# Which gate is worked out by seven products: one second gate goes back to the ordinary product, and the sums it needed are formed beside it

## The chip, the core and the metric

The kernel runs on one core of one Trainium2 chip. The metric is the time of one execution in microseconds (us) on the device. The core has a matrix engine, TensorE (PE in the profile, its weight loads PEld), a vector engine (DVE), a scalar engine (ACT), GpSimd (POOL) and SyncE (SP). Each works through its own instructions in a fixed order and waits for the others through semaphores. SP issues nearly all loads from memory here, in the order of its queue; POOL issues a few more.

## The reference, cut to what matters

One decoder layer on 512 tokens of width 1024. The normalised input `h` is projected to everything that three mixers need, and to three gates:

```
z, xbc, dt_raw, q, k, v, u, gates = split(h @ w_in)
y_ssd  = state_space_branch(z, xbc, dt_raw) @ w_ssd_out
y_attn = attention_branch(q, k, v) @ w_attn_out
y_pool = (multi_scale_pool(u, w_pool_mix) * pool_scale) @ w_pool_out
g_ssd, g_attn, g_pool = split(sigmoid(gates))
x = x + g1 * ((g_ssd * y_ssd + g_attn * y_attn + g_pool * y_pool) @ w_out)
x = x + g2 * (square(relu(norm(x) @ w_ff1)) @ w_ff2)
```

`multi_scale_pool` subtracts each value from its mean over the last 2, 4, 8 or 16 tokens (four groups of 256 channels) and multiplies each group by its own 256x256 matrix of `w_pool_mix`.

## The kernel before, in words

**Layout.** Activations lie with channels on the 128 partitions and the 512 tokens along the free axis; 1024 channels are eight such blocks. A product of 1024x512 weights with them is a chunk; each gate has two chunks, so GS, GA and GP (state-space, attention, pooled) have a first and a second gate each.

**Precision.** Every operand is a sum of a high part and a low part. ACT casts a weight tile to get the high part `wh` (L279 or L786), DVE subtracts to get the low part `wl` (L279 or L787), and PE forms three products: low by high, high by high, high by low (lines L293 to L295, or L811).

**An ordinary chunk** (`gemm_feat`) streams four weight tiles of 128x1024 through `wstream`; each serves two of the eight blocks. The loads go to a ring of four buffers (`raws`), the two parts to a ring of three pairs (`wsp`). A chunk is 8 blocks x 4 output blocks x 3 = 96 matmuls with 512 columns.

**A chunk by seven products** (`seven_products`) treats inputs, weights and tokens as 2x2 blocks and needs seven half-size products instead of eight: 7 x 4 x 2 x 3 = 168 matmuls with 256 columns. For it DVE also builds sums of weights (L793 to L796, into the buffers tagged L0, L1, N0, N1 of the pool `exp`, each of which exists once) and sums of the input (`input_sums`). The latter come in four pieces of work, each of two additions of whole blocks (L753, L754), four of half blocks (L755 to L758) and the split of the two results into high and low parts (L320 on ACT, L321 on DVE). The input sums are kept and serve every seven-product gate that follows.

**Side work.** What is not a chunk's own work waits in a list, `side`. After each weight tile of an ordinary chunk, and twice in a seven-product one, `tick` takes one entry from that list and emits it after that tile's two split instructions. `rest(n)` puts n empty entries in it, `call` one function, and `flush` empties it.

**The stretch in question.** After the attention branch the program forms the two chunks of `u` (`pool(0)`, `pool(1)`: the chunk, then the running means on DVE), then the state-space branch's first gate GS 0, its projection `project` with `w_ssd_out` chunk 0, its second gate GS 1, the second projection, and then both pooled gates GP 0 and GP 1 with theirs. `mix_weights(n)` loads two of the four 256x256 matrices into one `raws` buffer and splits them into the `exp` buffers L0, N0 (n = 0) or L1, N1 (n = 1). `pool_mix(gi)` multiplies group gi on PE (12 matmuls), scales it on ACT (L1141) and DVE (L1142), and POOL stores it in memory (L1146); `again` loads all of it back (L1263) once the blocks of the state-space branch have become free.

**What sets the order.** A scheduler orders each engine's instructions at build time, from the order in which the code emits them. Weight loads and splits are moved ahead by `high_priority(offset=AHEAD)`, evacuations by a smaller amount; nothing is reordered on the chip.

## Time and profile before

| what | us |
|---|---|
| median of 3 runs | 1106.65 (1105.22 to 1106.88) |
| the profiled execution | 1104.65 |
| span of its trace | 1102.9 |
| PE busy | 1087.0 (99%) |
| DVE busy | 761.6 (69%) |
| ACT busy | 536.9 (49%) |

The span runs from the first to the last recorded instruction of the profiled execution; the 1.75 us between 1102.9 and 1104.65 lie around it. Times inside the trace count from the start of the span. Matmuls are pipelined: a row's duration is its latency, and neighbours start closer together than that, so the pace is read from starts or from a stretch with its count. "Idle before" names what ended the wait ahead of an instruction.

### The profile page before, as it was taken

The page shows a single profiled execution, that of the slowest core. Times are in us where ns is not written, and L with a number is a line of the kernel's source. Part 1 is how long each engine was busy: PE and PEld are TensorE (multiplying, and loading weights), DVE is VectorE, ACT ScalarE, POOL GpSimd, SP SyncE. Part 2 cuts the span into 40 slices and gives each one's busy share as a digit, 9 for nine tenths or more (in the row PEclk, how much of TensorE's full clock was granted, in tenths as well). Part 3 has the DMA queues.
Part 4 walks back from the last instruction along what each step waited for, and adds up shares of the span by engine and source line. Part 5 has one row for each costly group of instructions (what it writes and reads, how often), then busy time and mean ns, then how long its engine had stood idle before and what let it go on. Part 6 is the DMA issues. An engine that isn't in the chain of part 4 may idle for free.

```text
span 1102.9 us, 15616 instructions
## 1 busy us (share of the span) xinstructions
PE 1087.0 (99%) x6022; PEld 937.8 (85%) x6022; DVE 761.6 (69%) x1441; ACT 536.9 (49%) x877; POOL 29.2 (3%) x58
## 2 busy tenths in 40 slices
PE   8999999999999999999988999999999999999998
PEld 7878888888887888888877899899889989989987
DVE  8955746683777956678777557476797587687664
ACT  8965864643545942835425245363344334335330
POOL 0000000000000000000110200000000000000000
PEclk9999999999999999999998999999999999999999
DMA  9723143555644342223534542560224134133032
GB/s 346 296 96 100 65 162 123 176 169 182 203 151 156 102 134 99 93 77 96 191 114 132 172 155 71 178 229 1 77 58 136 64 108 134 56 116 135 20 115 77
DMA packets 49230, 142.42 MB, mean 129 GB/s; under 512 B 5874, under 2 KB 6642, under 8 KB 49156
## 3 DMA queue, kind: packets, MB, share of 16 engines
q1 hardware_dynamic: 43088, 126.08, 34.5%
q0 software_dynamic: 5344, 14.16, 4.2%
q10 hardware_dynamic: 724, 1.18, 0.3%
q8 instruction: 47, 0.77, 0.3%
q14 instruction: 27, 0.22, 0.1%
HBM read 135.08 MB, written 6.32 MB: 128 GB/s over the span
## 4 chain that ended last, share of the span: by engine, by line
PE 79%; issue 16%; DVE 2%; DMA 1%; POOL 1%; ACT 0%; SPq 0%; POOLq 0%; DVEq 0%; ACTq 0%
PE psacc L293 18%; PE psacc L295 18%; PE psacc L294 18%; PE psacc L811 16%; PE psacc L533 4%; PE psS L612 1%; PE pso L728 1%; PE pso L726 1%; POOL pool L1146 1%; PE psqT L591 0%; PE pskT L596 0%; PE pspT L709 0%; DMA xT<-in_x_dram 0%; DMA pool<-pooll 0%; POOL M L1044 0%
## 5 line engine op out<-in xcount | busy, mean ns | idle before, releaser
L279 DVE TENSOR_TENSOR wl<-raw,wh 128x1024 fp32r<-128x1024 f32 x128 | 156.2, 1221 | 138.3 <-ACT wh L279 132.8
L279 ACT CAST wh<-raw 128x1024 fp32r<-128x1024 f32 x128 | 134.2, 1049 | 208.8 <-PE psacc L294 118.6
L293 PE MATMUL psacc<-hl,wh 128*128 128x512 f32 x320 | 128.8, 403 | 0.2 <-ACT pT L710 0.2
L294 PE MATMUL psacc<-hh,wh 128*128 128x512 f32 x320 | 124.6, 390 | 0.0
L295 PE MATMUL psacc<-hh,wl 128*128 128x512 f32 x320 | 124.5, 390 | 0.0
L293 PE MATMUL psacc<-al,wh 128*128 128x512 f32 (+1 forms) x260 | 100.4, 386 | 0.0
L294 PE MATMUL psacc<-ah,wh 128*128 128x512 f32 (+1 forms) x260 | 100.4, 386 | 0.0
L295 PE MATMUL psacc<-ah,wl 128*128 128x512 f32 (+1 forms) x260 | 100.3, 386 | 0.0
L293 PE MATMUL psacc<-wl,rh 128*128 128x512 f32 x192 | 77.4, 403 | 0.0
L295 PE MATMUL psacc<-wh,rl 128*128 128x512 f32 x192 | 75.2, 392 | 0.0
L294 PE MATMUL psacc<-wh,rh 128*128 128x512 f32 x192 | 75.2, 392 | 0.0
L293 PEld LDWEIGHTS psacc<-hl,wh 128*128 128x128 f32 x320 | 60.1, 188 | 13.4 <-issue 1.2
L294 PEld LDWEIGHTS psacc<-hh,wh 128*128 128x128 f32 x320 | 60.2, 188 | 13.3 <-issue 1.4
L295 PEld LDWEIGHTS psacc<-hh,wl 128*128 128x128 f32 x320 | 60.1, 188 | 12.9
L787 DVE TENSOR_TENSOR wl<-rawl,wh 128x512 fp32r<-128x512 f32 (+1 forms) x36 | 33.7, 954 | 35.6 <-ACT wh L786 35.6
L1441 DVE SCALAR_TENSOR_TENSOR xr<-psacc,modv,xr 128x512 f32<-128x512 f32 (+1 forms) x65 | 44.7, 738 | 18.7 <-PE psacc L295 18.7
L295 PEld LDWEIGHTS psacc<-ah,wl 128*128 128x128 f32 x260 | 48.8, 188 | 9.9
L293 PEld LDWEIGHTS psacc<-al,wh 128*128 128x128 f32 x260 | 48.9, 188 | 9.7
L294 PEld LDWEIGHTS psacc<-ah,wh 128*128 128x128 f32 x260 | 48.9, 188 | 9.6
L786 ACT CAST wh<-rawl 128x512 fp32r<-128x512 f32 (+1 forms) x36 | 29.2, 833 | 51.3 <-PE psacc L294 28.7
L786 ACT CAST wh<-wsum 128x1024 fp32r<-128x1024 f32 x18 | 19.0, 1053 | 72.0 <-PE psacc L294 69.5
L811 PE MATMUL psacc<-txl,wh 128*128 128x256 f32 x144 | 42.0, 292 | 4.4 <-DVE txl L321 4.4
(423 smaller groups left out, 2746.5 us busy)
## 6 DMA issues: line engine op xcount, KB each, us to landing
raw<-in_w_in_dram SPq DMA_DIRECT2D x74, 512.0 KB, 3.6
raw<-in_w_ff_dram SPq DMA_DIRECT2D x52, 512.0 KB, 3.8
wa<-in_w_ada_dram SPq DMA_DIRECT2D x64, 256.0 KB, 3.5
wada<-in_w_ada_dram SPq DMA_DIRECT2D x14, 512.0 KB, 7.8
rawl<-in_w_ff_dram SPq DMA_DIRECT2D x12, 512.0 KB, 3.5
wst<-in_w_in_dram SPq DMA_DIRECT2D x16, 256.0 KB, 7.8
M<-prow POOLq DMA_DIRECT2D x16, 256.0 KB, 3.7
raw<-in_w_ssd_out_dram SPq DMA_DIRECT2D x8, 512.0 KB, 3.6
```

The lines of the kernel that those rows point to most:

```text
L279: edges[:] = S.copy(wh, raw), V.tensor_tensor(wl, raw, wh.bitcast(F32), ALU.subtract)
L293: mm(ps, lhsT=wh, rhs=xl, start=first, stop=False)
L294: mm(ps, lhsT=wh, rhs=xh, start=False, stop=False)
L295: mm(ps, lhsT=wl, rhs=xh, start=False, stop=last)
L533: mm(ps[j], lhsT=t[:, j, :], rhs=w, start=first, stop=last)
L612: mm(so[b], lhsT=qT[:, b * P : (b + 1) * P], rhs=kT[:, (b + 1) * P - n : (b + 1) * P], start=True, stop=True)
L726: mm(od, lhsT=vs[kb][:, hs], rhs=pT[b // 2][:, cs : cs + P], start=(b == 0), stop=False, skip_group_check=True)
L728: mm(ov[:, b, :], lhsT=vs[b][:, hs], rhs=pT[0][:, b * P : (b + 1) * P], start=False, stop=(gi == 2 and b == 3), skip_group_check=True)
L786: S.copy(h, x)
L787: V.tensor_tensor(l, x, h.bitcast(F32), ALU.subtract)
L811: mm(o, lhsT=x[:, cs], rhs=y, start=first and k == 0 and j == 0 and n == 0, stop=k == 3 and n == 2, skip_group_check=True)
L1441: V.scalar_tensor_tensor(xT[d][:, ts], p[:, : ts.stop - ts.start], modv[:, 3, d : d + 1], xT[d][:, ts], ALU.mult, ALU.add)
```

## The change

The state-space branch's second gate becomes an ordinary chunk; the two pooled gates stay the only gates by seven products. The four pieces of input sums move from "between GS 0 and GS 1" to the four ticks of that ordinary chunk. Around it, the empty entries go, one of them stays, and the pooled branch's matrices and mixing are queued in another order.

```
-    for half in range(2):
-        call(mix_weights, half)
-        pool(half)
-        rest(2)
-        call(pool_mix, 2 * half)
-        if half == 0:
-            call(pool_mix, 1)
-    side.append(lambda: (pool_mix(3), sums[0]()))
-    side.extend(sums[1:])
+
+    pool(0)
+    call(mix_weights, 0)
+    pool(1)
+    call(pool_mix, 0)
+    side.append(lambda: (mix_weights(1), pool_mix(1)))
+    rest(1)
+    call(pool_mix, 2)
+    call(pool_mix, 3)
     sg = gate(GS, 0)
     project(a["w_ssd_out"], 8, 0, yh, yl, sg)
     flush()
-    sg = gate(GS, 1, tq)
+    side.extend(sums)
+    sg = gate(GS, 1)
     project(a["w_ssd_out"], 8, 1, yh, yl, sg)
+    flush()
```

What the scheduler makes of it is seen at three places. On PE, at the point where GS 1 begins (`psmix` and `psacc` are accumulators; `pdh`, `pdl` a group's means; `wmL`, `wmN` the parts of a mixing matrix; `ynh`, `ynl` the state-space result), before:

```order
L295 MATMUL psmix_5234<-pdh_4836,wmN_5088 128x512
L293 MATMUL psmix_5234<-pdl_4855,wmL_5087 128x512
L294 MATMUL psmix_5234<-pdh_4854,wmL_5087 128x512
L295 MATMUL psmix_5234<-pdh_4854,wmN_5088 128x512
L811 MATMUL psacc_5345<-hl_254,wh_5329 128x256
L811 MATMUL psacc_5345<-hh_246,wh_5329 128x256
```

The same six places now:

```order
L293 MATMUL psacc_5090<-ynl_4744,wh_5213 128x512
L294 MATMUL psacc_5090<-ynh_4743,wh_5213 128x512
L295 MATMUL psacc_5090<-ynh_4743,wl_5214 128x512
L293 MATMUL psacc_5249<-hl_254,wh_5255 128x512
L294 MATMUL psacc_5249<-hh_246,wh_5255 128x512
L295 MATMUL psacc_5249<-hh_246,wl_5256 128x512
```

The mixing of groups 2 and 3 stood right ahead of GS 1 and is gone from there: group 0 is now mixed after the first weight tile of GS 0, group 1 after its second, group 2 at its end, and group 3 after the first tile of the projection. The number of matmuls between the starts of GS 0 and GS 1 is the same, 240.

On SP, the loads from the third tile of the first projection on (`raw` and `rawl` with `in_w_in` behind GS 0 are gate weights; L777 loads the left half of a seven-product gate's weights into tags L0 and L1, L778 the right half), before:

```order
L286 DMA raw_5121<-in_w_ssd_out_dram 128x1024
L286 DMA raw_5151<-in_w_ssd_out_dram 128x1024
L778 DMA raw_5322<-in_w_in_dram 128x1024
L778 DMA raw_5326<-in_w_in_dram 128x1024
L777 DMA rawl_5321<-in_w_in_dram 128x1024
L286 DMA raw_5572<-in_w_ssd_out_dram 128x1024
L286 DMA raw_5602<-in_w_ssd_out_dram 128x1024
L777 DMA rawl_5325<-in_w_in_dram 128x1024
L777 DMA rawl_5732<-in_w_in_dram 128x1024
```

And now:

```order
L777 DMA rawl_5617<-in_w_in_dram 128x1024
L286 DMA raw_5211<-in_w_ssd_out_dram 128x1024
L286 DMA raw_5253<-in_w_in_dram 128x1024
L286 DMA raw_5301<-in_w_in_dram 128x1024
L286 DMA raw_5349<-in_w_in_dram 128x1024
L286 DMA raw_5397<-in_w_in_dram 128x1024
L777 DMA rawl_5621<-in_w_in_dram 128x1024
L286 DMA raw_5457<-in_w_ssd_out_dram 128x1024
L286 DMA raw_5487<-in_w_ssd_out_dram 128x1024
L286 DMA raw_5517<-in_w_ssd_out_dram 128x1024
L286 DMA raw_5547<-in_w_ssd_out_dram 128x1024
L778 DMA raw_5618<-in_w_in_dram 128x1024
```

The left half of GP 0's weights (5617, 5621) is now asked for a whole gate and projection ahead of its use; four ordinary tiles of GS 1 (5253 to 5397) stand where GS 1's halves stood.

On DVE, in the middle of the second gate's stretch, before:

```order
L787 TENSOR_TENSOR wl_5330<-rawl_5325,wh_5329 128x512
L794 TENSOR_TENSOR rawl_5325<-rawl_5325 128x2x256
L795 TENSOR_TENSOR wsum_5340<-wsum_5340,rawl_5325 128x2x256
L755 TENSOR_TENSOR tq_5269<-tq_5267 128x256
L796 TENSOR_TENSOR rawl_5325<-raw_5326,wsum_5340 128x2x256
L756 TENSOR_TENSOR tq_5269<-tq_5268,tq_5269 128x256
L787 TENSOR_TENSOR wl_5402<-wsum_5340,wh_5401 128x1024
```

And now, from the second tile of GS 1 on (`sg` is a gate; L884 multiplies it with the projection, L891 adds it to the sum of branches):

```order
L279 TENSOR_TENSOR wl_5304<-raw_5301,wh_5303 128x1024
L753 TENSOR_TENSOR tq_5331<-hh_247,hl_255 128x512
L754 TENSOR_TENSOR tq_5332<-hh_251,hl_259 128x512
L755 TENSOR_TENSOR tq_5333<-tq_5331 128x256
L884 TENSOR_TENSOR sg_5079<-psacc_5087,sg_5079 128x512
L884 TENSOR_TENSOR sg_5080<-psacc_5088,sg_5080 128x512
L884 TENSOR_TENSOR sg_5081<-psacc_5089,sg_5081 128x512
L884 TENSOR_TENSOR sg_5082<-psacc_5090,sg_5082 128x512
L891 TENSOR_TENSOR sg_3936<-sg_3936,sg_5079 128x512
L279 TENSOR_TENSOR wl_5352<-raw_5349,wh_5351 128x1024
L891 TENSOR_TENSOR sg_3937<-sg_3937,sg_5080 128x512
L891 TENSOR_TENSOR sg_3938<-sg_3938,sg_5081 128x512
```

Pieces of the input sums stood between the steps of the weights of GS 1; they now stand between the low parts of ordinary tiles, one piece behind each.

## The prediction

> **What bounds the kernel now.** I read the page's head first, then stretches of the trace (a table by stage), then the waits by engine, then the timelines of the stage that stands out.

> ```profile
> span 1102.9 us, 15616 instructions
> PE 1087.0 (99%) x6022; PEld 937.8 (85%) x6022; DVE 761.6 (69%) x1441; ACT 536.9 (49%) x877; POOL 29.2 (3%) x58
> PEclk9999999999999999999998999999999999999999
> ```

> PE is busy for 99% of the span, so the time is PE's matmuls plus its few gaps. One slice of 40 has a digit of 8 in the granted clock. The table by stage finds it (stretch, its length, then busy time and count by engine in the order PE, PEld, DVE, ACT, POOL, then granted clock and DMA):

> ```profile
> 515.03:542.20 27.17, 27.17 (x121) 22.52 (x120) 23.16 (x50) 13.41 (x19) 2.17 (x4) 1.00 0.43 136
> 542.20:569.87 27.67, 27.53 (x121) 22.45 (x120) 18.17 (x29) 7.31 (x11) 4.45 (x9) 1.00 0.32 115
> 569.87:604.43 34.56, 25.50 (x170) 23.92 (x169) 26.10 (x46) 15.94 (x24) 4.67 (x9) 0.85 0.47 152
> 604.43:626.38 21.95, 21.95 (x100) 18.18 (x99) 11.97 (x17) 6.09 (x10) 3.70 (x7) 1.00 0.67 192
> 626.38:646.70 20.32, 20.32 (x169) 20.20 (x169) 13.62 (x20) 10.57 (x16) 2.11 (x4) 1.00 0.60 183
> 646.70:668.50 21.80, 21.80 (x99) 18.04 (x98) 11.98 (x17) 6.06 (x10) 0.00 (x0) 1.00 0.22 72
> 668.50:688.80 20.30, 20.30 (x169) 20.21 (x169) 16.15 (x24) 12.76 (x20) 0.00 (x0) 1.00 0.25 88
> ```

> These are GS 0 with one mixing, the first projection with three, GS 1, the second projection, GP 0, the third projection, GP 1. (A count is a few over 96 or 168 where a neighbour's matmul reaches in.) The same 168 matmuls take 20.32 and 20.30 us in the pooled gates and 34.56 us in GS 1. There PE stands idle for 34.56 - 25.50 = 9.06 us, and the granted clock is 0.85. The waits, for all of PE's run (times, longest):

> ```profile
> PE psacc L811 <- DVE txl L321: 4.4, 2, 3.0
> PE psacc L811 <- ACT wh L786: 3.5, 2, 3.0
> PE psacc L811 <- DVE wl L787: 1.1, 2, 0.7
> ```

> These sum to 9.0 us: all of PE's waiting at L811 in the whole program lies in this one gate. Two causes stand behind them.

> ```profile
> SPq L777 <- PE psmix L295: 26.3, 2, 18.0
> 569.84 21.19 SPq L777 DMA_DIRECT2D rawl<-in_w_in_dram  x3
> 574.48 0.62 ACT L786 CAST wh<-rawl 128x512 fp32r<-128x512 f32 x1 [3.21 <-DMA rawl<-in_w_in_dram]
> 575.15 0.38 PE L811 MATMUL psacc<-hl,wh 128*128 128x256 f32 x1 [2.97 <-ACT wh L786]
> 576.97 0.41 PE L811 MATMUL psacc<-hh,wh 128*128 128x256 f32 x1
> 577.19 0.41 PE L811 MATMUL psacc<-hh,wl 128*128 128x256 f32 x1
> 585.95 0.28 PE L811 MATMUL psacc<-hl,wh 128*128 128x256 f32 x1
> 586.07 0.28 PE L811 MATMUL psacc<-hh,wh 128*128 128x256 f32 x1
> 594.04 0.39 PE L811 MATMUL psacc<-txl,wh 128*128 128x256 f32 x1 [3.00 <-DVE txl L321]
> ```

> First, the second left quarter-pair of GS 1 (tag L1) shares its buffer with a mixing matrix that the last `pool_mix` reads right up to the start of GS 1. SP can only issue that load at 569.84; it lands past 574, and cast, subtraction and PE follow. Second, the input sums are made at the same time as the weight sums, on one DVE, and PE arrives at `txl` before it is there (the 3.00 us at 594.04 and 1.4 more). In between the matmuls start 0.22 apart instead of 0.12: the clock is at half. The split of the gate at that clock:

> ```profile
> 569.87:575.15 5.28, 2.31 (x18) 2.10 (x18) 1.00 0.96 317
> 575.15:585.67 10.52, 8.87 (x38) 8.08 (x38) 0.52 0.11 42
> 585.67:604.43 18.76, 14.31 (x114) 13.69 (x113) 1.00 0.54 168
> ```

> So of the 14.24 us that GS 1 takes beyond GP 0, 9.06 are waits, and 25.50 - 20.32 = 5.18 are matmuls at a clock of 0.52.

> [...]

> **The change, part by part.** *The gate's product.* 168 matmuls of 256 columns go, 96 of 512 columns come. An ordinary chunk costs 21.80 us when nothing holds it (646.70 to 668.50; the stretch with mixing gives 96/120 x 27.17 = 21.7). The stage therefore goes from 34.56 to 21.80 us: **-12.76 us**. Against an undisturbed seven-product gate the ordinary one would be 1.48 us dearer (21.80 - 20.32), so the whole gain is stall and clock.

> *The mixing.* Its 48 matmuls move, none is added. Between the start of GS 0 (515.03) and that of GS 1 (569.87) stand 240 matmuls as before, so GS 1 begins at the same time if none of them waits. Groups 0 and 1 need means and matrices that are there before 515. Groups 2 and 3 need what ends here:

> ```profile
> 523.09 0.69 DVE L321 TENSOR_TENSOR pdl<-win,pdh 128x512 fp32r<-128x512 f32 x1
> 530.13 1.23 DVE L1130 TENSOR_TENSOR wmN<-wmix,wmL 128x1024 fp32r<-128x1024 f32 x1
> 537.78 0.69 DVE L321 TENSOR_TENSOR pdl<-win,pdh 128x512 fp32r<-128x512 f32 x1 [0.74 <-ACT pdh L320]
> ```

> Group 2 is mixed at 542.2 now; its matrix, behind one low part and one evacuation more on DVE, is there by about 535 (my estimate from these rows). Group 3 comes 24 + 12 matmuls later, at 550.4; its last mean was ready at 538.5 and comes 1 to 2 us later. Cover: 7 and 10 us, so nothing. The accumulators of the first projection are, as before, the two that mixing has just left; the 0.14 us of PE idle in 542.20 to 569.87 stay.

> *The sums.* Their cost on DVE and ACT does not change; their place does. From here the costs are the printed durations, which are upper bounds, since neighbours overlap.

> ```profile
> L754 DVE TENSOR_TENSOR tq<-hh,hl x4: 678/681/683, 542.6 to 582.3; 128x512 f32<-128x512 f32 x4
> L755 DVE TENSOR_TENSOR tq<-tq x4: 416/417/419, 551.6 to 591.5; 128x256 f32<-128x256 f32 x4
> L321 DVE TENSOR_TENSOR txl<-tq,txh x4: 679/682/691, 570.1 to 593.3; 128x512 fp32r<-128x512 f32 x4
> 602.71 1.23 DVE L279 TENSOR_TENSOR wl<-raw,wh 128x1024 fp32r<-128x1024 f32 x1
> 625.66 0.68 DVE L891 TENSOR_TENSOR sg<-sg,r 128x512 f32<-128x512 f32 x1
> raw<-in_w_in_dram SPq DMA_DIRECT2D x74, 512.0 KB, 3.6
> ```

> A piece is 4 x 0.68 + 4 x 0.42 = 4.4 us of DVE. In the 21.8 us of GS 1 DVE has three pieces (13.2; the first fits before, while DVE is idle behind tiles), four low parts (4.9) and the end of the first projection (eight operations of 0.68, 5.4): 23.5, a little more than the stage. What decides is how far the low parts are ahead, since each stands behind a piece. I walked DVE's queue from 569.9. The third tile's low part follows five operations of 0.68: ready 574.5, used by PE two tiles of 5.45 us later, 580.8. The fourth: ready 580.4, used 586.2. The second projection's first: ready 586.7, used 591.7; its second: 592.3 against 597.1; its third stands behind an addition for GP 0 that waits for a load, issued when the second is done and 3.6 us under way: 592.3 + 3.6 + 2 x 0.68 + 1.23 = 598.5 against 602.6. The smallest lead is 4.1 us. I cost it at nothing; without that cover each piece would cost PE its 4.4 us. ACT's casts wait in the same rhythm for `txh` inputs, and each has 1.05 us within these leads.

> *SP and POOL.* GS 1's four tiles are the same 2 MB. Their buffers come free with the low parts of the tiles four places earlier, and the L0 and L1 loads ahead of them wait for mixing that now ends at 531 and 553. The stored groups leave POOL earlier. Their reload still waits for the blocks of the second gate:

> ```profile
> 632.22 0.53 POOL L1263 DMA_DIRECT2D pooll<-pool  x1 [1.31 <-issue]
> ```

> The last one was issued at 632.22 and used from 646.70. Both shift with the second projection, and the 14 us stay. The empty entries cost no instruction, so removing them is free. GP 0 now finds both halves and all sums long made, as GP 1 did.

> **Sum.** 1104.65 - 12.76 = 1091.9 us for a profiled execution. The profiled one lay 2.00 us under the median of the runs, so against the median: 1106.65 - 12.76 = **1093.9 us**, a ratio of 0.988. About 0.2% (2.2 us) is what a measurement of this kernel can tell from no change.

> **Rivals.** *Part of the stall survives (0.10).* A low part or a sum is late once in GS 1 or GP 0. For it: DVE's 23.5 us in a 21.8 us stage. Against: leads of 4.1 us and more. Price: one wait like those seen, 3.0 us, alone or with 5.2 of half clock: 1096.9 to 1102.1.

> *The clock falls anyway (0.03).* If the 0.52 did not come from those waits, only they go: -12.76 + 5.18 = -7.58, 1099.1. For it: 2.97 us dropped the clock and 3.00 us did not. Against: no other stretch above has a clock below 1.00. [...]

> *The stall is the first seven-product gate's, and moves to GP 0 (0.04).* Then GS 1 costs 21.80 and GP 0 34.56: +1.48, 1108.1, within 0.2%. For it: whatever gate comes first must wait for fresh sums. Against: the sums end about 590 now, GP 0 starts about 613, and L1 is free at 553.

> *Slower: DVE becomes the bound (0.03).* In GS 1 and the projection behind it each low part stands behind a piece. If the ring of three pairs gave no lead, PE would wait 4.4 us at each of four tiles and run at half clock for a while: 17.6 + 5.2 - 12.76 = +10, 1116.7; without the clock 1111.5. It decides once the third tile's low part is later than 580.8, 6 us behind my walk.

> **How the numbers follow.** The forecast has 0.80, with an own range of 1092.5 to 1095.5. If the 2 us by which timed runs exceed the profiled one lie in this stall, the gain is up to 14.8 (1091.9). The range of 1091.3 to 1098.5 leaves out most of the first rival's upper half, the others, and a tail of the forecast. Faster: 0.80 + 0.10 + 0.03 = 0.93; within 0.2%: 0.04; slower: 0.03.

> **What would show it.** Right: the stage after the first projection lasts 21.8 us with PE idle near 0 and a clock of 1.00; no wait of PE at L811 is left; GP 0 starts near 613.5 and takes 20.3; every later stage starts 12.8 earlier; the page's slices show no 8 in the clock; PE's busy time falls by about 3.7 (25.50 to 21.80). Wrong: waits of PE at L293 or L295 for `wl` of L279 behind L753 to L758 (DVE the bound), at `psmix` for `pdl` (mixing too early), or at L811 for `txl` or `wh` in GP 0 (the stall moved).

## The result, and the profile after

The changed kernel takes **1092.96 us** (median of 4 runs, 1092.29 to 1093.08) where the kernel before takes 1105.93 in the same comparison (4 runs, 1104.63 to 1106.88): a ratio of **0.9882, 95% interval 0.9865 to 0.9899**. Predicted was 1093.9 with a range of 1091.3 to 1098.5. The profiled execution went from 1104.65 to 1092.29 us, 12.36 less; the forecast was 12.76.

The page's head after, with the granted clock in its 40 slices:

```profile
span 1090.5 us, 15439 instructions
PE 1082.6 (99%) x5950; PEld 931.6 (85%) x5950; DVE 750.8 (69%) x1421; ACT 530.7 (49%) x865; POOL 29.2 (3%) x58
PEclk9999999999999999999999999999999999999999
```

The 8 is gone. The table by stage (stretch, length, busy time and count of PE, PEld, DVE, ACT, POOL, then clock and DMA): GS 0, first projection, GS 1, second projection, GP 0, third projection, GP 1.

```profile
514.40:541.56 27.16, 27.16 (x121) 22.48 (x120) 23.71 (x51) 10.40 (x16) 4.32 (x8) 1.00 0.52 180
541.56:570.30 28.74, 27.51 (x121) 22.41 (x120) 14.72 (x22) 10.79 (x15) 4.30 (x8) 1.00 0.50 178
570.30:592.07 21.77, 21.77 (x97) 18.02 (x96) 19.68 (x34) 9.30 (x13) 2.67 (x5) 1.00 0.51 153
592.07:614.00 21.93, 21.93 (x99) 18.19 (x98) 10.07 (x14) 5.00 (x8) 3.69 (x7) 1.00 0.47 138
614.00:634.20 20.20, 20.20 (x169) 20.08 (x169) 13.62 (x20) 10.53 (x15) 2.12 (x4) 1.00 0.59 183
634.20:656.00 21.80, 21.80 (x99) 18.03 (x98) 11.95 (x17) 5.97 (x10) 0.00 (x0) 1.00 0.21 73
656.00:676.20 20.20, 20.20 (x169) 20.11 (x168) 16.28 (x25) 12.83 (x19) 0.00 (x0) 1.00 0.24 86
```

GS 1 went from 34.56 to 21.77 us, with PE busy throughout at full clock, and the stages behind it keep their lengths. (The table's stretches begin up to 0.2 us beside the stages; by PE's starts GP 0 takes 20.33 us in both kernels.) One stage got longer: the first projection, 28.74 instead of 27.67, with 1.23 us in which PE is idle. All waits of PE that remain:

```profile
PE pssx L411 <- DVE sq L420: 1.4, 1, 1.4
PE psacc L293 <- DVE pooll L1142: 1.2, 1, 1.2
PE pswarm L404 <- DVE ones L373: 1.1, 1, 1.1
PE psrx L465 <- DVE diag L462: 0.3, 1, 0.3
PE psacc L293 <- ACT pT L710: 0.2, 1, 0.2
```

None is at L811 any more; the one on `pooll` is new, and the others belong to the kernel's start and its attention branch. The new wait, step by step in the timeline (an end in brackets: idle before, and what ended it):

```profile
536.18 0.54 POOL L1146 DMA_DIRECT2D pool<-pooll  x1 [0.72 <-DVE pooll L1142]
541.32 1.28 ACT L332 ACT_TABLE_LOAD   x1 [4.17 <-DMA pool<-pooll]
545.49 1.28 ACT L1141 ACTIVATE poolh<-psmix,vec 128x512 fp32r<-128x512 f32 x2
546.23 1.41 DVE L1142 SCALAR_TENSOR_TENSOR pooll<-psmix,vec,poolh 128x512 fp32r<-128x512 f32 x2 [0.82 <-ACT poolh L1141]
547.03 0.50 PE L293 MATMUL psacc<-ynl,wh 128*128 128x512 f32 x1 [1.23 <-DVE pooll L1142]
```

The projection's third output block needs an accumulator that the mixing of group 2 has just filled. That accumulator is emptied late: ACT stood idle for 4.17 us until a store of an earlier group of the pooled branch had landed (issued by POOL at 536.18; these stores take 2.3 to 6.8 us from issue to landing, 5.4 at the median), because GS 0's gate values are written into buffers that the store still read. Only then came the table of the sigmoid, the four gate blocks, and the pooled block behind them. In the kernel before the same table load waited less:

```profile
538.63 1.28 ACT L332 ACT_TABLE_LOAD   x1 [0.89 <-DMA pool<-poolh]
```

The account of the profiled executions, by the starts of PE's matmuls: GS 1 gives -12.80 (34.56 to 21.76), GS 0 and the first projection take +1.11 together (54.84 to 55.95), and the changed kernel's trace reaches GS 0 0.67 us earlier (515.03 to 514.36). Of these 0.67 us, 0.65 are there already 5.7 us into the trace, far ahead of anything that the change touches, and two traces of the changed kernel differ by 0.38 us as well where PE reaches 481. Together -12.36, as measured. That the new wait and the earlier start nearly cancel is chance.

### The profile page after: what moved, and what is told of

It is laid out like the page before. It is cut to its first block, busy times and chain, and to the rows that moved or that the text cites. A ratio compares the mean times of both kernels' runs of the same rounds, so it can differ in the third digit from the quotient of the medians.

```text
span 1090.5 us, 15439 instructions
## 1 busy us (share of the span) xinstructions
PE 1082.6 (99%) x5950; PEld 931.6 (85%) x5950; DVE 750.8 (69%) x1421; ACT 530.7 (49%) x865; POOL 29.2 (3%) x58
## 4 chain that ended last, share of the span: by engine, by line
PE 97%; DVE 1%; ACT 0%; DMA 0%; issue 0%; SPq 0%; DVEq 0%; ACTq 0%
PE psacc L293 23%; PE psacc L295 23%; PE psacc L294 23%; PE psacc L811 15%; PE psacc L533 4%; PE psS L612 1%; PE psy L1064 1%; PE pso L728 1%; PE psyo L1072 1%; PE pso L726 1%; PE psqT L591 0%; PE pskT L596 0%; PE psst L1023 0%; PE pspT L709 0%; DMA xT<-in_x_dram 0%; PE psX L1012 0%
## 5 line engine op out<-in xcount | busy, mean ns | idle before, releaser
L279 DVE TENSOR_TENSOR wl<-raw,wh 128x1024 fp32r<-128x1024 f32 x132 | 161.2, 1221 | 150.1 <-ACT wh L279 140.5
L279 ACT CAST wh<-raw 128x1024 fp32r<-128x1024 f32 x132 | 138.4, 1049 | 213.9 <-PE psacc L294 121.0
L293 PE MATMUL psacc<-hl,wh 128*128 128x512 f32 x352 | 141.2, 402 | 0.2 <-ACT pT L710 0.2
L294 PE MATMUL psacc<-hh,wh 128*128 128x512 f32 x352 | 137.1, 389 | 0.0
L295 PE MATMUL psacc<-hh,wl 128*128 128x512 f32 x352 | 137.0, 390 | 0.0
L293 PE MATMUL psacc<-al,wh 128*128 128x512 f32 (+1 forms) x260 | 100.4, 386 | 0.0
L295 PE MATMUL psacc<-ah,wl 128*128 128x512 f32 (+1 forms) x260 | 100.3, 386 | 0.0
L293 PEld LDWEIGHTS psacc<-hl,wh 128*128 128x128 f32 x352 | 66.1, 188 | 14.7 <-issue 1.2
L294 PEld LDWEIGHTS psacc<-hh,wh 128*128 128x128 f32 x352 | 66.2, 188 | 14.5 <-issue 1.4
L295 PEld LDWEIGHTS psacc<-hh,wl 128*128 128x128 f32 x352 | 66.1, 188 | 14.1
L293 PE MATMUL psacc<-wl,rh 128*128 128x512 f32 x192 | 77.4, 403 | 0.0
L295 PE MATMUL psacc<-wh,rl 128*128 128x512 f32 x192 | 75.2, 392 | 0.0
L295 PEld LDWEIGHTS psacc<-ah,wl 128*128 128x128 f32 x260 | 48.8, 188 | 9.9
L293 PEld LDWEIGHTS psacc<-al,wh 128*128 128x128 f32 x260 | 48.9, 188 | 9.7
L787 DVE TENSOR_TENSOR wl<-rawl,wh 128x512 fp32r<-128x512 f32 (+1 forms) x32 | 29.9, 954 | 34.3 <-ACT wh L786 34.3
L786 ACT CAST wh<-wsum 128x1024 fp32r<-128x1024 f32 x16 | 16.9, 1054 | 64.1 <-PE psacc L294 64.1
L786 ACT CAST wh<-rawl 128x512 fp32r<-128x512 f32 (+1 forms) x32 | 25.9, 833 | 43.2 <-PE psacc L294 26.0
L293 PEld LDWEIGHTS psacc<-wl,rh 128*128 128x128 f32 x192 | 36.1, 188 | 7.7 <-ACT qT L592 0.5
## 6 DMA issues: line engine op xcount, KB each, us to landing
raw<-in_w_in_dram SPq DMA_DIRECT2D x76, 512.0 KB, 3.6
raw<-in_w_ff_dram SPq DMA_DIRECT2D x52, 512.0 KB, 3.8
wada<-in_w_ada_dram SPq DMA_DIRECT2D x14, 512.0 KB, 7.8
rawl<-in_w_ff_dram SPq DMA_DIRECT2D x12, 512.0 KB, 3.5
raw<-in_w_ssd_out_dram SPq DMA_DIRECT2D x8, 512.0 KB, 3.6
```

What stands on the lines that cost most here:

```text
L279: edges[:] = S.copy(wh, raw), V.tensor_tensor(wl, raw, wh.bitcast(F32), ALU.subtract)
L293: mm(ps, lhsT=wh, rhs=xl, start=first, stop=False)
L294: mm(ps, lhsT=wh, rhs=xh, start=False, stop=False)
L295: mm(ps, lhsT=wl, rhs=xh, start=False, stop=last)
L786: S.copy(h, x)
L787: V.tensor_tensor(l, x, h.bitcast(F32), ALU.subtract)
```

## The experiments

Each short diff is against the kernel named. "Before" in a result is the kernel before, run on the same chip beside it.

### Which edit carries the gain

**The gate alone.** The kernel before, with only GS 1 made an ordinary chunk; mixing and sums stay where they were.

```
-    sg = gate(GS, 1, tq)
+    sg = gate(GS, 1)
```

> The kernel before with one edit: the state-space branch's second gate as an ordinary chunk. Mixing and input sums stay where they stood. Theory (the loss was the stall inside the seven-product gate and nothing else): the gate takes 21.8 us, no wait of PE at L811 is left, and all of the gain comes with this edit alone: 1105.9 - 12.8 = 1093.1 us, the changed kernel within 0.2%. Rival (the new order of mixing and sums is needed too): the sums, which now queue on DVE ahead of the ordinary tiles' low parts and wait for blocks that mixing still holds, make PE wait 3 to 6 us in this gate or in GP 0: 1096 to 1099 us.

Measured: 1091.91 us (1091.54 to 1093.69), before 1105.13, ratio 0.9886 [0.9869, 0.9902]. Its only wait in the stretch:

```profile
PE psacc L293 <- DVE pooll L1142: 0.2, 1, 0.2
```

There is no wait at L811, and the gate takes 21.76 us (569.60 to 591.36 by PE's starts). So one line of the diff carries the whole gain. The new order of mixing and sums adds nothing to it; it brings the wait at the accumulators, 1.2 us against 0.2 here. The runs of the two kernels overlap, so that last point rests on the traces.

### What the stall of GS 1 was made of

Four kernels keep seven products in GS 1 and take away one cause at a time.

**Early mixing, late sums (first form).** The change's order of the mixing, the sums queued behind it and beside the first projection, GS 1 by seven products. Against the kernel before the mixing is queued as in the change, and

```
+    call(pool_mix, 3)
+    side.extend(sums)
     sg = gate(GS, 0)
```

> The changed kernel's order of mixing, but the state-space branch's second gate by seven products again, with the four pieces of sums beside the first projection. Theory (two causes, the shared buffer L1 and the late sums, made the stall): both are gone, the gate takes 20.3 us as GP 0 does, 1.5 us less than the ordinary one: 1092.96 - 1.5 = 1091.5 us, slightly better than the changed kernel. Rival (a seven-product gate with fresh sums always stalls, since DVE cannot make both kinds of sums in time): PE waits 3 us or more at txl, and the clock may fall: 1094.5 to 1100 us.

Measured: 1095.79 us (1095.17 to 1096.3), ratio 0.9915 [0.9901, 0.993]. GS 1 and its one wait:

```profile
571.72:595.21 23.49, 20.62 (x169) 20.25 (x168) 18.69 (x30) 11.32 (x16) 2.66 (x5) 1.00 0.42 133
581.68 0.38 PE L811 MATMUL psacc<-txl,wh 128*128 128x256 f32 x1 [2.87 <-DVE txl L321]
```

This is the rival's case (1094.5 to 1100). With the mixing early no load is late. A sum still is, by 2.87 us, and the clock stays full through that wait.

**Early mixing, late sums (second form).** The same, with the sums queued only behind the first projection.

```
     project(a["w_ssd_out"], 8, 0, yh, yl, sg)
+    side.extend(sums)
     flush()
     sg = gate(GS, 1, tq)
```

> The changed kernel's order of mixing, three gates by seven products as before, and the sums emitted where they were, after the first projection. It takes away the shared buffer's wait alone. Theory (additive causes): the wait for the load of L1 (3.0 us and the 1.6 us of short waits behind it) and the half clock go, the 4.4 us for the sums stay: 1105.9 - 9.8 = 1096.1 us. Rival 1 (the causes hide one another): PE comes to the sums earlier and waits there longer, so most of the gain is lost: 1100 to 1104 us. Rival 2 (the sums were late only because blocks and the load were): no wait is left, 1091.5 us.

Measured: 1096.38 us (1095.52 to 1096.97), ratio 0.992 [0.9906, 0.9935]. The number is that of the account that adds the parts up; the trace is not. GS 1 in three stretches, and its two waits of over half a microsecond:

```profile
570.60:580.70 10.10, 8.23 (x64) 7.61 (x63) 10.10 (x16) 4.35 (x6) 0.00 (x0) 1.00 0.01 2
580.70:584.20 3.50, 3.50 (x19) 3.50 (x18) 3.12 (x6) 1.14 (x2) 0.00 (x0) 0.51 0.39 114
584.20:595.30 11.10, 10.98 (x91) 10.78 (x91) 7.49 (x12) 6.79 (x10) 2.67 (x5) 1.00 0.70 236
```

```profile
577.61 0.39 PE L811 MATMUL psacc<-hh,wl 128*128 128x256 f32 x1 [0.57 <-DVE wl L787]
579.42 0.39 PE L811 MATMUL psacc<-txl,wh 128*128 128x256 f32 x1 [1.30 <-DVE txl L321]
```

The waits fell to 1.9 us, not to the 4.4 that was expected to stay, and 3.5 us at a clock of 0.51 came in their place, which the account had put down to the late load.

**Late mixing, no wait for sums.** The kernel before, but in GS 1 the seven products take single blocks of the input in place of sums of two, so this gate's values are not the reference's; all else is computed. The sums are formed beside the second projection.

```
-    side.append(lambda: (pool_mix(3), sums[0]()))
-    side.extend(sums[1:])
+    call(pool_mix, 3)
...
-    sg = gate(GS, 1, tq)
+    sg = gate(GS, 1, [((hh[k], hl[k]), (hh[k + 4], hl[k + 4])) for k in range(4)])
+    side.extend(sums)
```

> The kernel before, with GS 1 by seven products, but its sums of two blocks of the input are not waited for: the high and low parts of single blocks stand in their place, so this gate's values are not the reference's, and all else is computed. The sums are formed beside the second projection instead, for the pooled gates. The late mixing ahead of GS 1, and with it the late load of tag L1, stays. This asks how much of the stall is the load alone. If the parts of the stall add up (2.97 us and about 1.6 us of short waits, and the half clock that follows them, are the load's; 4.4 us the sums'), GS 1 takes 34.56 - 4.4 = about 30 us and the time is about 1100.6. If the half clock cost hardly any time because the vector engine's sums set the pace behind it (as the run with filled wait showed), the 5.2 us of half clock are now on the path, since nothing covers them: the same 1100. If without the sums the gaps are too short for the clock to fall, GS 1 takes 20.3 + 4.6 = 25 us and the time is about 1095.5.

Measured: 1096.19 us (1095.56 to 1096.66), before 1104.87, ratio 0.9922 [0.9907, 0.9937]. GS 1, and its waits:

```profile
569.31:596.16 26.85, 24.04 (x170) 23.08 (x168) 15.69 (x24) 12.03 (x17) 1.99 (x4) 0.87 0.54 177
```

```profile
PE psacc L811 <- ACT wh L786: 2.4, 1, 2.4
PE psacc L811 <- DVE wl L787: 0.3, 1, 0.3
```

Of the three cases named, none fits whole. Near the third in time, it had the fall of the clock that the third did without. The late load alone costs 26.85 - 20.37 = 6.5 us (20.37 is an undisturbed seven-product gate, below). The trace shows 2.7 us of waits and 6.8 us at half clock in it. How much the half clock adds is not settled: one of the four runs had a mean clock of 1.00 and took 1095.56 us, only 0.4 to 1.1 us less than the other three at 0.996 and 0.997. With the sums out of DVE's way, the waits behind the load are shorter too: 2.7 us for `wh` and `wl`, where the kernel before has 3.5 + 1.1 = 4.6.

**The load's wait filled with work.** The kernel before, with 14 matmuls into an accumulator that nobody reads, put ahead of the place where PE waited 2.97 us for the load.

```
             for k, (wh, wl) in enumerate(ws, k0):
+                if fill and k == 2:
+                    spare = psm("fill")
+                    for n in range(fill):
+                        mm(spare, lhsT=xh[0][:, :P], rhs=xh[1], start=True, stop=True)
+                    free(spare)
```

> The kernel before, with 14 extra matmuls of 512 columns into a bank of their own (their results are not used) put into the state-space branch's second gate where PE waited 2.97 us for the load. They take 14 x 0.227 = 3.2 us. If the half clock came from the waits, the clock stays at 1.00. Additive account (9.06 us of waits plus 5.18 us of slow matmuls): 5.2 - 0.2 = 5.0 us less, 1100.9 us. By the chain of waits (only the slow matmuls from 580.6 to 586.4, 27 of them, lie on the chain; the rest runs beside DVE): 27 x (0.214 - 0.120) = 2.5 us less, 1103.4 us. If the clock falls whatever PE does: 1106 us, and slow matmuls in the trace.

Measured: 1104.37 us (1103.33 to 1105.89, 10 runs), before 1105.13 (13 runs), ratio 0.999 [0.9981, 1.0]. GS 1 in three stretches:

```profile
569.80:581.80 12.00, 9.03 (x55) 7.46 (x55) 10.09 (x18) 4.42 (x7) 2.04 (x4) 1.00 0.53 175
581.80:585.00 3.20, 3.20 (x18) 3.20 (x17) 3.20 (x8) 1.20 (x2) 0.00 (x0) 0.52 0.03 5
585.00:603.85 18.85, 14.40 (x115) 13.83 (x115) 12.87 (x22) 10.21 (x15) 2.66 (x5) 0.99 0.52 167
```

```profile
593.46 0.39 PE L816 MATMUL psacc<-txl,wh 128*128 128x256 f32 x1 [2.99 <-DVE txl L321]
```

(L816 is L811 there.) The fall of the clock near 575 is gone, so the long wait for the load had brought it (the ten runs have a mean clock of 0.995 to 0.998, the kernel before beside them 0.992 to 0.995). A later one came in its place, behind waits of 0.81 and 0.85 us. The half clock shrank to 3.4 us from 10.2, and the gate became 0.6 us shorter (34.00 by PE's starts, 569.85 to 603.85). The wait for the last sum ends at 593.46, where it ended at 594.04 before, and is as long as ever. So in the kernel before DVE set the pace of this gate (it is busy for 10.04 of the 10.24 us of half clock): whatever PE lost to the clock in the middle, it would otherwise have lost waiting for the sums. Neither the account that adds the parts (1100.9) nor the one with a chain (1103.4) gave this.

The parts side by side, seven products in all of them:

| GS 1 | us | beyond 20.37 | PE's waits | half clock lasts |
|---|---|---|---|---|
| before: late mixing, late sums | 34.56 | 14.2 | 9.06 | 10.2 us |
| before, load's wait filled | 34.00 | 13.6 | 7.4 beside the filling | 3.4 us |
| late mixing, no wait for sums | 26.85 | 6.5 | 2.7 | 6.8 us |
| early mixing, late sums | 23.49, 24.64 | 3.1, 4.3 | 2.9, 1.9 | none, 3.4 us |
| early mixing, early sums | 20.38, 20.37 | 0 | 0 | none |

The causes do not add: the late load alone costs 6.5, late sums alone 3.1 or 4.3, and both together 14.2. The other way round, either cure alone gives back 7.7 or 9.9 to 11.1 of the 14.2. The sums are not equally late in all of these kernels, so the parts are prices of each as it was built. Late mixing with early sums was not tried.

### The wait at the accumulators

**One empty entry more.** The change, with groups 2 and 3 mixed one weight tile later.

```
-    rest(1)
+    rest(2)
```

> The changed kernel with two empty entries instead of one, so that groups 2 and 3 are mixed one weight tile later, after the first and second tile of the first projection. Theory (the 1.23 us that PE waits in the changed kernel at the start of the first projection is an accumulator that the mixing has just used and whose evacuation is late): the projection then takes accumulators that were free long before, the wait goes, 1.2 us less: 1091.8 us, level with the kernel that only has the ordinary gate. Rival (the wait is late evacuation on ACT and DVE and moves to the mixing): no change, 1093.0 us. A measurement tells 1 us only roughly; the trace's wait decides.

Measured: 1090.84 us (1090.71 to 1091.79), before 1104.95, ratio 0.9873 [0.9859, 0.9888]. A second time, beside the change itself on one chip:

> The change with two empty entries in place of one ahead of the mixing of group 2. If what was seen before holds: 1090.9 us, 2 us under the change. If only the 1.2 us wait at the accumulators goes: 1091.7. If the earlier difference was chance: 1092.9.

Measured: 1091.08 us (1091.03 to 1091.15), ratio 0.9876 [0.9861, 0.9891]. There GS 1 starts at 569.13, against 570.56 in the change's trace beside it, and takes 21.76. The wait on `pooll` is gone, and so is ACT's wait for the store:

```profile
536.55 0.54 POOL L1146 DMA_DIRECT2D pool<-pooll  x1 [0.72 <-DVE pooll L1142]
537.59 1.28 ACT L332 ACT_TABLE_LOAD   x1
540.09 0.60 ACT L332 ACTIVATE sg<-psacc 128x512 f32<-128x512 f32 x1 [1.22 <-PE psacc L295]
```

No idle time stands before the table load, against 4.17 us. The store is no earlier: it is issued at 536.55, against 536.18 in the change, where ACT could go on only at 541.32; here ACT writes the first gate block at 540.09. The gate blocks lie in other buffers. Buffers are handed out in the order of the code, and group 2 no longer takes its four ahead of them; now its own blocks come behind that store, long after its issue: ahead of the first, at 548.93, ACT waits 0.54 us, and for PE. So an empty entry, which costs no instruction, gained 1.5 us (1092.61 to 1091.08). From the first mixing in GS 0 to the start of GS 1 PE takes 50.37 us in the change beside it (520.19 to 570.56) and 48.96 here (520.17 to 569.13), so the wait accounts for 1.41 of them. That is more than the 1.1 us of idle time listed for it there, because idle time counts only from the modelled end of the matmul before. The entry moves the mixing and frees ACT at once; which of the two would have been enough was not tried.

### How far DVE is from being the bound

**Longer sums.** The change, with `more` needless additions of whole blocks in each piece of the sums: 4 (some 2.4 us of DVE more per piece), then 7 (some 4.2).

```
                 t1, t2, x, y = (blk("tq") for _ in range(4))
+                for _ in range(more):
+                    V.tensor_tensor(t2, xh[k].bitcast(F32), xl[k].bitcast(F32), ALU.add)
```

> The changed kernel with four more additions of 128x512 in each piece of sums (repeated writes of one temporary, results unchanged): 4 x 0.60 = 2.4 us more of DVE per piece. By the leads that the prediction walked with full durations (5.8, 5.0, 4.8, 4.1 us), the second projection's second and third tile come late by 2.4 to 3 us: 1095.5 to 1096.5 us. By the leads read in the changed kernel's trace (8.5, 8.4, 8.4, 6.8 us): no wait or under 1 us: 1093.0 to 1094 us.

> The same with seven more additions per piece, 4.2 us, so that the sums cost twice as much. By the trace's leads the second projection's first tile is just in time and its second 4 us late: PE waits 4 to 7 us in all, 1097 to 1100 us, at L293 for wl of L279. By the prediction's walk: 8 to 12 us, 1101 to 1105 us. If the cover is larger than both say: 1093 us.

Measured: 1092.89 us (1092.73 to 1093.46), ratio 0.9891 [0.9876, 0.9906], with four, and 1092.94 (1092.87 to 1093.35), ratio 0.9892 [0.9875, 0.9908], with seven. Neither has a wait of PE for a low part or at L811; the only wait in this stretch is the change's, on `pooll`. With seven, GS 1 and the second projection:

```profile
570.00:592.00 22.00, 22.00 (x99) 18.22 (x98) 22.00 (x37) 6.40 (x8) 0.00 (x0) 1.00 0.30 101
592.00:614.00 22.00, 22.00 (x99) 18.22 (x98) 21.97 (x38) 7.91 (x12) 4.77 (x9) 1.00 0.51 146
```

DVE is busy without a break for 44 us, and PE does not wait. The rows of DVE show why:

```profile
583.42 1.22 DVE L279 TENSOR_TENSOR wl<-raw,wh 128x1024 fp32r<-128x1024 f32 x1
L755 DVE TENSOR_TENSOR tq<-hh,hl x4: 684/688/691, 562.8 to 609.0; 128x512 f32<-128x512 f32 x4
```

The low part at 583.42 is for a tile that PE takes up near 592, some 8 us later. (L755 is the first addition of a piece there; the lines are shifted by two.) The scheduler kept the low parts ahead and let the sums slide: the last piece starts at 609.0, where the change starts it at 580.3. GP 0 starts near 614, so this cover was nearly used up.

### A version that beats both

**Seven products in all three gates.** The change, with the mixing of group 2 ahead of the empty entry, the sums behind it, and GS 1 by seven products again.

```
-    rest(1)
     call(pool_mix, 2)
-    call(pool_mix, 3)
+    rest(1)
+    side.append(lambda: (pool_mix(3), sums[0]()))
+    side.extend(sums[1:])
...
-    side.extend(sums)
-    sg = gate(GS, 1)
+    sg = gate(GS, 1, tq)
```

> Three gates by seven products, with mixing of group 2 after the third tile of the first gate, of group 3 after the first tile of the first projection, and the four pieces of sums in that projection's four ticks, one tile (5.4 us) earlier than in the second experiment, which still waited 2.9 us for txl and 1.5 us for an accumulator. If lateness of the sums is all that is left: both waits go, the gate takes 20.3 us: 1095.8 - 4.4 = 1091.4 us, and 1.5 us less than the changed kernel. If DVE has no room for sums and weight sums between the two gates however they are placed: the wait for txl stays between 1.5 and 3 us: 1093 to 1094.5 us.

Measured: 1089.73 us (1089.48 to 1092.42), before 1104.95, ratio 0.9867 [0.9852, 0.9882]. One of its four runs took 1092.42 us at a mean clock of 0.996, where the others have 1.00; it was not profiled. Then once more, on one chip with the change and with the empty entry added:

> The changed kernel once more, on one chip with the two variants that looked faster. 1092.9 us, ratio 0.988.

> All three second and pooled gates by seven products, with the pooled branch's matrices and mixing queued early and the input sums beside GS 0 and the first projection. If what was seen before holds: 1089.7 us, ratio 0.9867, about 3 us under the change, of which 1.5 are the shorter gate (20.3 against 21.8) and 1.2 the wait at the accumulators. If that was chance: 1091.4 (the shorter gate alone) or 1092.9 (nothing).

| one chip, before 1104.87 us | median us | lowest to highest | ratio, 95% interval |
|---|---|---|---|
| the change | 1092.61 | 1092.48 to 1093.13 | 0.9891 [0.9876, 0.9906] |
| the change, one empty entry more | 1091.08 | 1091.03 to 1091.15 | 0.9876 [0.9861, 0.9891] |
| seven products in three gates | 1089.63 | 1089.36 to 1091.16 | 0.9868 [0.9851, 0.9884] |

In the last, GS 1 is an undisturbed seven-product gate:

```profile
568.73:589.10 20.37, 20.37 (x169) 20.20 (x168) 16.91 (x26) 10.70 (x15) 2.66 (x5) 1.00 0.48 153
```

No wait of PE at L811 or for `pooll` is left. It is 2.98 us under the change: 1.39 from the gate (21.76 to 20.37) and 1.41 from the wait at the accumulators (50.37 to 48.96, as above); 0.2 are not assigned. So the seven products were not to blame for the stall. The load and the sums came too late for this one gate, and could be had earlier.

## Why the prediction was right, point by point

*What bounds the kernel.* Right: PE's path, with one gate that stalls. The gain is that gate's, as the run with the gate alone shows.

*The gate's product, -12.76.* 34.56 became 21.77, so -12.79. The ordinary chunk's price, taken from the third projection, fitted to 0.03 us.

*The mixing, nothing.* **Mis-sized.** The step said "the 0.14 us of PE idle in 542.20 to 569.87 stay"; 1.23 us were measured there. Means and matrices came in time, as worked out. What it left out was the way out of the accumulators: group 2 is now mixed just ahead of a projection that needs its two accumulators a few matmuls later, and ACT, which empties them, stood behind a store that POOL issues. It followed SP's loads and POOL's reload, and not the buffers that POOL's stores hold.

*The sums, nothing.* Right in the result, and too timid in the working. The smallest lead was put at 4.1 us; the trace has low parts ready 6.7 to 8.6 us ahead of PE. Four and seven additions more per piece changed nothing, where by the walk a piece longer by 4.2 us should have used up that lead. The walk kept the printed order of DVE fixed and added durations up. The printed durations overlap, as it said itself; and with longer sums the order isn't kept. Its steps from one low part to the next, 5.9 and 6.3 us, are also longer than a piece and a low part by its own figures (4.4 + 1.23 = 5.6).

*SP and POOL, nothing.* Right for the loads: GP 0 and GP 1 keep their lengths, and nothing at L811 waits.

*The sum.* Against the profiled execution -12.76 stood for -12.36 measured, the difference being the +1.11 around the mixing and, by chance, 0.67 less ahead of GS 0. Against the median it started from 1106.65, the median of three runs; the comparison's own was 1105.93. With that start the same sum gives 1093.17, 0.2 us from the result.

*The rivals.* Part of the stall survived nowhere in GS 1 or GP 0; the wait of 1.23 us that did appear was in neither of its places. The clock did not fall: 1.00 in every stage. The stall did not move: GP 0 takes 20.3 us from 613.83. DVE is further from being the bound than that rival had it (the third tile's low part was ready at 573.0, where 580.8 was to decide); with 4.2 us more per piece there was still no wait.

*How the stall was split.* The split into 9.06 of waits and 5.18 of half clock is a true account of where PE's time went, and no account of what each cause costs. The second rival used it that way ("only they go: -7.58"), and so did the expectations of three runs. Filling the wait that brought the clock down gained 0.6 us in the gate. The granted clock fell at 575.52, behind the one wait of 2.97 us that ended at 575.15 and ahead of the next, of 0.73 us, that ended at 576.38. The split did no harm to the forecast, which replaced the whole gate.

*What would show it.* GS 1 near 21.8 at a clock of 1.00, no L811 waits, GP 0 near 613.5 (613.83): all as listed. "Every later stage 12.8 earlier" is 12.4 (626.21 to 613.83 for GP 0). PE's busy time fell by 4.4 instead of 3.7; 3.73 of that is GS 1 (25.50 to 21.77), the rest lies outside it and was not followed.

## What to carry to other kernels

Split a stall by what ends each wait to find its causes, and price a cure by what is late next: here the two causes cost 6.5 and 3.1 to 4.3 us alone and 14.2 together, and half clock in a stretch that another engine paces cost almost nothing (6.8 us less of it gained 0.6 us in the gate). When a producer is moved, follow its result until the accumulator is empty again; the engine that empties it may stand behind a store that has nothing to do with it. Before an edit replaces a stalling operation by a dearer one that doesn't stall, try to have its inputs made earlier: that was worth 1.4 us in the gate here, and 3 us together with the wait at the accumulators.

## What the runs showed of the hardware that was not expected

The stretches at half clock differ in length. In the kernel before it is 10.24 us: narrow stretches of the trace have a granted clock of 0.50 from 575.52 to 585.76, and of 1.00 on both sides. In the other traces the length follows from the mean clock of wider stretches: 6.8 us with no wait for sums (0.66 from 576.00 to 586.00), 3.4 us with the wait filled (0.52 from 581.80 to 585.00, 0.96 from there to 588.50) and 3.4 us in the second form (0.51 from 580.70 to 584.20). The first two are about three and two times as long as the others; why is not shown.

PE's busy time just ahead does not tell either. Here it is, from the rows of the traces, in 3.41 us (a third of the 10.24) up to each fall, and in as much up to the end of each of the three waits of about 3 us that left the clock alone. In the traces other than the first a fall is placed to 0.1 us, where the matmuls' starts go from 0.12 us apart to 0.21.

| trace | stretch, us | PE busy in it, us | clock after it |
|---|---|---|---|
| before | 572.11 to 575.52 | 0.44 | 0.50 |
| no wait for sums | 572.51 to 575.92 | 0.91 | 0.50 |
| wait filled | 578.49 to 581.90 | 1.76 | 0.50 |
| second form | 577.34 to 580.75 | 1.83 | 0.50 |
| before | 590.63 to 594.04 | 0.41 | 1.00 |
| wait filled | 590.05 to 593.46 | 0.42 | 1.00 |
| first form | 578.27 to 581.68 | 0.53 | 1.00 |

```profile
572.11:575.52 3.41, 0.44 (x3) 0.30 (x2) 1.72 (x4) 0.62 (x1) 0.27 (x1) 1.00 0.95 375
575.52:585.76 10.24, 8.59 (x38) 7.87 (x37) 10.04 (x20) 3.91 (x6) 0.00 (x0) 0.50 0.07 28
590.63:594.04 3.41, 0.41 (x4) 0.20 (x2) 3.40 (x10) 1.24 (x2) 0.54 (x1) 1.00 0.69 239
576.00:586.00 10.00, 9.86 (x57) 9.31 (x56) 5.01 (x7) 5.25 (x8) 0.00 (x0) 0.66 0.01 2
```

(Three lines of the kernel before, and one of the kernel with no wait for sums.) So PE was busy for half of the time ahead of two falls, and for an eighth of it where the clock did not fall; what decides is not shown. Nor did the clock rise as soon as PE was busy again: with no wait for sums PE was busy for 9.86 of the 10.00 us from 576.00, and 6.8 us of them were at half clock.

The spread of the kernel before goes with its clock: its longest runs, 1106.94 to 1107.51 us, have a mean clock of 0.992 where those of 1104 to 1105 have 0.995. The first four runs of the changed kernel lie within 0.8 us, at 1.00. This fits the longer runs having a longer half clock in GS 1; none of the longest was profiled.
